# A float32 transformer kernel under a list schedule: nine landing buffers for weight blocks instead of four, other cost estimates in the planner, and mixer 1's constants asked for later

## The chip, the cores and the metric

The kernel runs on one core of one Trainium2 chip. The metric is the device time of one execution in microseconds; the figure for a kernel is the median of its runs. TensorE multiplies matrices, VectorE, ScalarE and GpSimd do the rest of the arithmetic, and SP (SyncE) issues all transfers from the chip's memory.

## The reference

The input is `x` of 256 tokens by 1024 columns, float32. Two transformer blocks follow each other. The first is a feed-forward layer (`ffn1`, gate and up of 1024 x 2816 each, silu, down 2816 x 1024), a token mixer (`mixer1`: one projection `w_in`, sliding-window attention with sinks, a pooled branch over windows of 2, 4, 8 and 16 tokens, one projection `w_out`), and a second feed-forward layer (`ffn2`). The second block is a mixer of a state-space branch (SSD) and a latent attention branch (MLA) (`mixer2`), an attention over a memory of 256 tokens (`memory`), and a feed-forward layer with a short convolution (`conv_ffn`). RMS norms stand between all of them.

```python
for l in range(DEPTH):
    h = swiglu(rms_norm(x, ffn1_pre[l]), ffn1_w_gu[l], ffn1_w_down[l])
    x = x + 0.5 * rms_norm(h, ffn1_post[l])
    h = token_mixer(rms_norm(x, mix_pre[l]), cos, sin, w_in[l], w_pool[l], ...)
    x = x + rms_norm(h, mix_post[l])
    ...
```

Some 165 MB of weights are read once each.

## The kernel before, in words

**Numbers as pairs.** A matrix product in float32 is made of three products of `float32r` numbers: each operand is split into a high part (rounded to float32r) and a low part (what is left), and high x high, high x low and low x high are added in PSUM (`mm3`, L688, and `projB`, L1074). Operands are 128 x 1024 tiles.

**Weight blocks.** `wblock` (L655) brings in one block, at most 1024 float32 a partition (512 KB): it takes a landing tile of the class `raw`, SP loads the block into it, ScalarE copies it into a high tile of the class `w` (a CAST in the profile), and VectorE subtracts to make the low tile, again of class `w` (a TENSOR_TENSOR 128x1024). When VectorE has done so, the landing tile is free. `wblocks` (L674) does this for a whole matrix strip. In the start (first strip of `ffn1`) the pieces are smaller (`CUTS`): four for gate and three for up, 256 KB each but the last, with the four loads of the transposed input `xT` (256 KB each) between.

**A planner orders everything.** The layers do not issue instructions; they call a `Plan` object, which records them as nodes with their reads and writes (`add`, L228). `schedule` (L303) is a list scheduler: it keeps an estimated time for each engine, and again and again takes the instruction that can start first, in program order among equals. `cost` (L279) estimates an instruction's duration, `HOP` (L198) the time until another engine sees the result. The result is one fixed order for each engine; `issue` (L456) writes the instructions out in that order. On the chip each engine goes through its own list in order and waits for what the next instruction needs. Some copies and scalings may run on ScalarE or VectorE; the planner chooses by its estimates.

**Buffers.** Tiles belong to classes with a fixed number of slots (`SLOTS`, L27): `w` (128 x 1024 float32, 35 of them), `raw` (the landing tiles, 4), `s` (128 x 512), `tiny`, and `ps` (8 PSUM banks). A tile gets a slot when its first instruction is scheduled and gives it back after its last. The `w` tiles also hold the transposed activations, the heads of the attention, the states, and constants such as the post-norm gains. `RESERVE` and `AHEAD` keep later tiles from taking the slots that earlier ones need; `CAP` (L31) is the most `w` tiles that weight blocks may hold in a stage. SP alone is scheduled strictly in program order: in the planner's loop it never passes a load whose slot is not there yet.

```python
if s is None:
    if e == "SP":
        break
    continue
```

**Mixer 1** (`mixer1`, L948) begins by asking for its constants: two loads of the pooling band (`band`, 512 and 256 KB), the pool weights (256 KB), the pool scale and the post-norm gain (spread over all partitions, 256 and 512 KB). They go to four `w` tiles. Three small VectorE operations prepare the sinks, the attention mask and a bf16 identity. Then come the ten blocks of `w_in` (two for key and value, four for query, four for the pool branch), the products for both halves of 128 tokens, the attention, the pool branch, the norms, and `w_out` (`down`, L765, which runs the second half of the tokens four blocks behind the first).

**Norms.** A norm's factor is a power of -0.5 of a [128, 1] tile on GpSimd (`rsq`, L709, and `rstd`, L722); ScalarE or VectorE scales with it.

Of the kernel before, what the change touches and what calls it, by code (L numbers as in the profile page):

```python
# [25 lines left out]
BLK = 1024  # L26
SLOTS = {"w": 35, "raw": 4, "s": 14, "tiny": 24, "ps": 8}  # L27
RESERVE = {"w": 4, "weights": 4, "raw": 0, "s": 3, "tiny": 6, "ps": 2}
AHEAD = {"w": 24, "weights": 4, "raw": 1000, "s": 24, "tiny": 60, "ps": 24}
CUTS = (2, 4, 6, 8), (2, 4, 8)  # L30
CAP = {"start": 22, "ffn": 22, "mix": 16, "mix2": 16, "cffn": 22}  # L31
LAG = {"ffn1": 4, "mix1": 4, "ffn2": 4, "mix2": 4, "mem": 4, "cffn": 4}
# [91 lines left out]
class View:  # L124
# [26 lines left out]
    def bitcast(self, dtype):  # L151
        return self.then(self.ix, "bitcast", dtype)

    def real(self):
        r = self.tile.real
        for op, *a in self.ops:
            if op == "get":
                r = r[a[0]]
            elif op == "rearrange":
                r = r.rearrange(a[0], **a[1])  # L160
            else:
                r = getattr(r, op)(a[0])
        return r
# [33 lines left out]
TABLES = {"Silu": 1, "Sin": 1, "Exp": 2, "Tanh": 2}  # L197
HOP = {"PE": 190.0, "ACT": 190.0, "DVE": 190.0, "POOL": 190.0, "SP": 0.0}  # L198

# [11 lines left out]
class Plan:  # L211
# [66 lines left out]
    @staticmethod  # L278
    def cost(attr, op, a, k):  # L279
        out = k.get("out", a[0] if a else None)  # L280
        size = lambda v: int(np.prod(v.shape[1:]))
        ps = any(isinstance(v, View) and v.tile.cls == "ps" for v in list(a) + list(k.values()))
        if attr == "tensor":
            if op == "transpose":
                return 109.0
            n, dt = size(out), k["rhs"].tile.dtype
            if dt == F32R:
                return 4.0 + (0.4453 * n if n >= 256 else 4 * n / 2.4)
            return 5 + max(n, P) / 2.4 * (4 if dt == F32 else 1)
        if attr == "sync" or op == "dma_start":  # L290
            n = int(np.prod(out.shape)) * 4
            return max(n / 355.0, 470.0)
        if attr == "scalar":
            return 0.833 * size(out) + 94 + (93 if "accum_out" in k else 0)
        if attr == "vector":
            if op == "reduce_max":
                return 1.04 * size(a[1]) + 70
            one = op in ("tensor_copy", "tensor_scalar") and not ps
            return (0.52 if one else 1.04) * size(out) + (130 if ps else 70)
        return 1.05 * size(out) * (2 if out.tile.dtype == F32R else 1) + 464  # L300


    def schedule(self):  # L303
# [65 lines left out]
        while left:  # L369
# [36 lines left out]
            if n.alts[e][1] == "dma_start":  # L406
                T[e] = st + (1000.0 if e == "POOL" else 60.0)
                T["BUS"] = max(T["BUS"], st) + c
                n.end = max(T["BUS"], st) + 2000
            else:  # L410
                if e == "ACT" and n.func is not None and n.func != table:
                    c += 1300 if table is not None else 0
                    table = n.func
                if e == "PE" and st > T[e] + 30:
                    c += min(213.0, c)
                T[e] = n.end = st + c
            for x in n.alts:
                known[x].remove(n)
            for t in n.tiles:
# [7 lines left out]
                else:  # L427
                    t.slot = 0
            vis = n.end + HOP[e]
            for t in n.tiles:  # L430
# [6 lines left out]
            for u in n.users:  # L437
                same = e in u.alts and len(u.alts) == 1
                u.ready = max(u.ready, n.end + (0.0 if e == "PE" and same else 130.0 if same else HOP[e]))
                u.wait -= 1  # L440
                if u.wait == 0:
                    see(u)
# [122 lines left out]
class K:  # L565
# [89 lines left out]
    def wblock(self, src):  # L655
        nc = self.nc
        _, ka, nb = src.shape
        n = ka * nb
        raw = nc.tile("raw", [P, BLK], F32)
        nc.sync.dma_start(raw[:, :n], src.rearrange("p k n -> p (k n)"))  # L660
        nc.cap = CAP[self.phase]
        hi, lo = self.w1024(F32R), self.w1024(F32R)
        nc.scalar.copy(hi[:, :n], raw[:, :n])
        nc.vector.tensor_sub(lo[:, :n], raw[:, :n], hi.bitcast(F32)[:, :n])
        nc.cap = 0
# [282 lines left out]
    def mixer1(self, xT, nxt):  # L948
        nc, a = self.nc, self.a
        self.phase = "mix"  # L950
        band = [self.w1024(), self.w1024()]
        nc.sync.dma_start(band[0], a["band"][:, :1024])
# [4 lines left out]
        psc = self.bc(pw[:, 512:], a["pool_scale"][0])  # L957
        sink = self.rows[:, :8]
        nsink = self.const("nsink", [P, 8])
        nc.vector.tensor_scalar(nsink, sink, -1.0, None, op0=ALU.mult)  # L960
        mask = self.const("mask", [P, 256], BF16)
        nc.vector.tensor_copy(mask, self.cst[:, C_SWA : C_SWA + 256])
        idb = self.const("idb", [P, P], BF16)
        nc.vector.tensor_copy(idb, self.ident)
        post = self.bc(self.w1024(), a["mix_post"][0])

        w = "w_in"
        wkv = self.wblocks(w, KD, 1024, 1280)
        wq = self.wblocks(w, KD, 512, 1024)
        wu = self.wblocks(w, KD, 0, 512)  # L970
        kvs, us, qTs = self.w1024(), self.w1024(), self.w1024()
# [644 lines left out]
```

## Time and profile before

| | |
|---|---|
| median of the runs | 1002.12 us (3 runs, 1001.24 to 1003.1) |
| profiled execution, its own time | 1004.54 us |
| profiled execution, its span | 1002.8 us, 16342 instructions |
| TensorE busy | 974.9 us (97%) |
| VectorE busy | 710.4 us (71%) |
| ScalarE busy | 519.6 us (52%) |
| GpSimd busy | 38.9 us (4%) |
| read from memory | 165.37 MB, 166 GB/s over the span |

Nearly every instruction has the same line, L469, which is where `issue` writes them all out; so the profile is read by engine, operation, shape and time, not by line. In a row of the timeline, the number in brackets is the idle time of the engine before the instruction, with what ended it. DVE is VectorE, ACT ScalarE, POOL GpSimd, PE TensorE, SPq the queue of SP.

### The profile page before, as it was taken

The numbers are of one execution on the slowest core, as the hardware profiler recorded it, in microseconds if no ns is written. First come the engines' busy times: TensorE is split into PE (matmuls) and PEld (weight loads), VectorE is DVE, ScalarE is ACT, GpSimd is POOL, SyncE is SP. The second block draws the span as 40 slices with busy tenths as digits, with TensorE's granted clock in tenths as the row PEclk, the third lists the DMA queues.
The fourth block names the chain that finished last, engine by engine and source line by source line (L and its number), as shares of the span: only waits on it lengthen the run. The fifth ranks groups of instructions, "written<-read, shape, count | busy, mean of one in ns | idle before, by whom it ended". The sixth has DMA issues, their size and how long they took to land.

```text
span 1002.8 us, 16342 instructions
## 1 busy us (share of the span) xinstructions
PE 974.9 (97%) x6437; PEld 882.1 (88%) x6437; DVE 710.4 (71%) x1201; ACT 519.6 (52%) x846; POOL 38.9 (4%) x52
## 2 busy tenths in 40 slices
PE   7999999999999999999999999999999999999997
PEld 6999998877889999888988987877997899999885
DVE  5878554567686656446999999998637698888542
ACT  5756324357455434244766666465535367555331
POOL 0100000000010000001200000111000000000000
PEclk9999999999999999999999999999999999999999
DMA  7877554455158555554444545035656056556351
GB/s 243 286 245 250 162 180 146 179 187 194 40 169 286 168 170 156 165 164 135 147 159 132 168 129 208 1 104 168 217 163 230 24 168 230 172 197 207 122 166 42
DMA packets 49421, 167.48 MB, mean 167 GB/s; under 512 B 5824, under 2 KB 7360, under 8 KB 49344
## 3 DMA queue, kind: packets, MB, share of 16 engines
q1 hardware_dynamic: 49344, 166.44, 51.3%
q8 instruction: 50, 0.82, 0.3%
q14 instruction: 27, 0.22, 0.1%
HBM read 165.37 MB, written 1.05 MB: 166 GB/s over the span
## 4 chain that ended last, share of the span: by engine, by line
PE 75%; DVE 9%; DMA 7%; ACT 4%; issue 3%; POOL 1%; SPq 0%; POOLq 0%; ACTq 0%; DVEq 0%
PE t L469 75%; DVE t L469 9%; ACT t L469 4%; DMA t<-in_w_in_from_dram 3%; DMA t<-in_ffn_w_gu_from_dram 2%; POOL t L469 1%; DMA t<-in_w_out_from_dram 1%; DMA t<-in_xT_dram 1%; SPq L469 0%; DMA t<-in_mla_w_kv_up_from_dram 0%; ACT L469 0%; POOLq L1612 0%; ACTq L469 0%; DVEq L469 0%; POOLq L469 0%
## 5 line engine op out<-in xcount | busy, mean ns | idle before, releaser
L469 PE MATMUL t<-t,t 128*128 128x256 f32 (+6 forms) x6428 | 971.4, 314 | 19.9 <-DVE t L469 11.2
L469 PEld LDWEIGHTS t<-t,t 128*128 128x128 f32 (+2 forms) x6412 | 880.0, 187 | 109.9 <-DVE t L469 16.4
L469 DVE TENSOR_TENSOR t<-t,t 128x1024 fp32r<-128x1024 f32 (+13 forms) x792 | 581.7, 777 | 240.6 <-PE t L469 121.2
L469 ACT CAST t<-t 128x1024 fp32r<-128x1024 f32 (+5 forms) x406 | 359.9, 903 | 313.1 <-PE t L469 146.6
L469 ACT ACTIVATE t<-t 128x512 bf16<-128x512 f32 (+10 forms) x132 | 72.8, 557 | 126.1 <-DVE t L469 88.7
L469 ACT ACTIVATE t<-t,t 128x256 f32<-128x256 f32 (+4 forms) x143 | 69.5, 516 | 26.0 <-POOL t L469 10.8
L469 DVE SCALAR_TENSOR_TENSOR t<-t,t,t 128x254 f32<-128x254 f32 (+5 forms) x158 | 68.6, 493 | 16.9 <-ACT t L469 12.8
L469 POOL TENSOR_TENSOR t<-t,t 128x1 f32<-128x1 f32 x38 | 33.4, 879 | 954.7 <-DVE t L469 954.7
L469 DVE CAST t<-t 128x512 fp32r<-128x512 f32 (+9 forms) x55 | 22.1, 407 | 7.8 <-PE t L469 4.7
L469 ACT COPY t<-t 128x256 f32<-128x256 f32 (+3 forms) x34 | 14.7, 446 | 12.9 <-PE t L469 12.7
L469 DVE TENSOR_SCALAR t<-t,t 128x128 f32<-128x128 f32 (+7 forms) x33 | 10.1, 317 | 14.0 <-POOL t L469 4.5
L469 DVE TENSOR_REDUCE t<-t 128x2 f32<-128x512 f32 (+1 forms) x22 | 14.4, 682 | 0.1
L469 DVE COPY t<-t 128x256 f32<-128x256 f32 (+5 forms) x27 | 13.0, 483 | 0.6 <-PE t L469 0.5
L469 DVE TENSOR_SCALAR t<-t 128x1 f32<-128x1 f32 (+5 forms) x69 | 10.1, 157 | 4.1 <-ACT t L469 2.9
L469 ACT ACTIVATION_READ_ACCUMULATOR t<-t 128x1 f32 x60 | 11.4, 190 | 0.0
L469 ACT ACTIVATION_READ_ACCUMULATOR t<-t,t 128x1 f32 x48 | 10.1, 211 | 0.0
L469 ACT ACT_TABLE_LOAD x7 | 9.0, 1283 | 1.4 <-PEq L1604 0.7
L469 DVE SCALAR_TENSOR_TENSOR t<-t,t 128x512 f32<-128x512 f32 (+2 forms) x17 | 9.2, 544 | 0.6 <-ACT t L469 0.4
L469 DVE RECIPROCAL t<-t 128x2 f32<-128x2 f32 (+2 forms) x23 | 4.0, 173 | 2.8 <-ACT t L469 2.6
L469 PEld LDWEIGHTS <-t 128*128 128x128 bf16 x25 | 2.3, 112 | 3.6 <-issue 2.1
L469 POOL COPY t<-t 128x8 f32<-128x8 f32 (+1 forms) x6 | 4.7, 810 | 4.2 <-DMA t<-in_cst_dram 3.8
L469 PE MATMUL t<-t 128*128 128x512 bf16 x9 | 3.4, 557 | 1.2 <-DVE t L469 1.2
(10 smaller groups left out, 8.1 us busy)
## 6 DMA issues: line engine op xcount, KB each, us to landing
t<-in_ffn_w_gu_from_dram SPq DMA_DIRECT2D x85, 512.0 KB, 4.9
t<-in_ffn_w_down_from_dram SPq DMA_DIRECT2D x44, 512.0 KB, 4.1
t<-in_w_ffn_up_from_dram SPq DMA_DIRECT2D x44, 512.0 KB, 4.3
t<-in_w_in_from_dram SPq DMA_DIRECT2D x34, 512.0 KB, 4.5
t<-in_w_out_from_dram SPq DMA_DIRECT2D x24, 512.0 KB, 4.5
t<-in_w_ffn_down_from_dram SPq DMA_DIRECT2D x22, 512.0 KB, 4.7
t<-in_w_mem_k_from_dram SPq DMA_DIRECT2D x8, 512.0 KB, 4.4
t<-in_w_mem_q_from_dram SPq DMA_DIRECT2D x8, 512.0 KB, 4.5
```

Source lines behind the costliest of these rows:

```text
L469: getattr(getattr(nc, attr), op)(*[real(v) for v in a], **{x: real(v) for x, v in k.items()})
```

## The change

The landing class grows from 4 to 9 tiles and `w` shrinks from 35 to 33; the cap on weight tiles goes from 22 to 20 in the start and in the feed-forward stages. The last hunk takes a scratch area for descriptors down to 1024 bytes, which no transfer of this kernel uses, and so makes room. `HOP` becomes a table by producer and consumer, and `cost` gets other constants: a scalar operand adds to a VectorE or ScalarE operation, PSUM operands are cheaper, a transfer is 413 bytes a nanosecond instead of 355, an issue on SP 420 ns instead of 60, the penalty for a gap on TensorE is gone, and a [128, 1] operation on GpSimd is 550 ns. In `mixer1` the `w_in` blocks are asked for first and the five constant loads after them. `wblock` uses a view of the landing tile in place of the tile; its instructions stay the same. The `dtype` of a view now sees a bitcast, so that the planner tells float32 products from float32r ones.

```diff
-SLOTS = {"w": 35, "raw": 4, "s": 14, "tiny": 24, "ps": 8}
+SLOTS = {"w": 33, "raw": 9, "s": 14, "tiny": 24, "ps": 8}
...
-CAP = {"start": 22, "ffn": 22, "mix": 16, "mix2": 16, "cffn": 22}
+CAP = {"start": 20, "ffn": 20, "mix": 16, "mix2": 16, "cffn": 20}
...
-HOP = {"PE": 190.0, "ACT": 190.0, "DVE": 190.0, "POOL": 190.0, "SP": 0.0}
+
+HOP = {
+    "PE": {"PE": 0.0, "ACT": 200.0, "DVE": 200.0, "POOL": 240.0, "SP": 240.0},
+    "ACT": {"PE": 155.0, "ACT": 140.0, "DVE": 133.0, "POOL": 180.0, "SP": 180.0},
+    "DVE": {"PE": 140.0, "ACT": 118.0, "DVE": 125.0, "POOL": 166.0, "SP": 166.0},
+    "POOL": {"PE": 55.0, "ACT": 33.0, "DVE": 33.0, "POOL": 40.0, "SP": 55.0},
+    "SP": {"PE": 50.0, "ACT": 30.0, "DVE": 30.0, "POOL": 30.0, "SP": 0.0},
+}
...
-            n, dt = size(out), k["rhs"].tile.dtype
+            n, dt = size(out), k["rhs"].dtype
...
-            return 5 + max(n, P) / 2.4 * (4 if dt == F32 else 1)
-        if attr == "sync" or op == "dma_start":
-            n = int(np.prod(out.shape)) * 4
-            return max(n / 355.0, 470.0)
+            return 2 * max(4 + 0.8906 * n, 109.0) if dt == F32 else 4 + 0.4453 * n
+        if op == "dma_start":
+            return max(int(np.prod(out.shape)) * 4 / 413.0, 300.0)
         if attr == "scalar":
-            return 0.833 * size(out) + 94 + (93 if "accum_out" in k else 0)
+            scalars = sum(isinstance(v, View) for v in (k.get("scale"), k.get("bias"), a[2] if op == "mul" else None))
+            return 0.833 * size(out) + (58 if ps else 94) + 88 * scalars + (98 if "accum_out" in k else 0)
...
-            return (0.52 if one else 1.04) * size(out) + (130 if ps else 70)
-        return 1.05 * size(out) * (2 if out.tile.dtype == F32R else 1) + 464
+            scalars = op in ("tensor_scalar", "scalar_tensor_tensor") and any(isinstance(v, View) for v in (a[2], a[3] if op == "tensor_scalar" else None))
+            return (0.52 if one else 1.04) * size(out) + 70 + 60 * scalars
+        return 550.0 if size(out) == 1 else 1.05 * size(out) + 464
...
-                T[e] = st + (1000.0 if e == "POOL" else 60.0)
+                T[e] = st + 420.0
...
-                if e == "PE" and st > T[e] + 30:
-                    c += min(213.0, c)
...
-            vis = n.end + HOP[e]
+            vis = n.end + 170.0
...
-                same = e in u.alts and len(u.alts) == 1
-                u.ready = max(u.ready, n.end + (0.0 if e == "PE" and same else 130.0 if same else HOP[e]))
+                u.ready = max(u.ready, n.end + max(HOP[e][x] for x in u.alts))
...
     def mixer1(self, xT, nxt):
         nc, a = self.nc, self.a
         self.phase = "mix"
+        sink = self.rows[:, :8]
+        nsink = self.const("nsink", [P, 8])
...
+        wkv = self.wblocks(w, KD, 1024, 1280)
+        wq = self.wblocks(w, KD, 512, 1024)
+        wu = self.wblocks(w, KD, 0, 512)
         band = [self.w1024(), self.w1024()]
         nc.sync.dma_start(band[0], a["band"][:, :1024])
...
         post = self.bc(self.w1024(), a["mix_post"][0])
-
-        w = "w_in"
-        wkv = self.wblocks(w, KD, 1024, 1280)
-        wq = self.wblocks(w, KD, 512, 1024)
-        wu = self.wblocks(w, KD, 0, 512)
...
-    nc = _bacc.Bacc("TRN2", target_bir_lowering=False, num_devices=1)
+    nc = _bacc.Bacc("TRN2", target_bir_lowering=False, num_devices=1, dynamic_dma_scratch_size=1024)
```

## Rows read from the trace of the kernel before

**Rows 1.** The page, busy us, share of the span and instructions by engine.

```profile
PE 974.9 (97%) x6437; PEld 882.1 (88%) x6437; DVE 710.4 (71%) x1201; ACT 519.6 (52%) x846; POOL 38.9 (4%) x52
```

**Rows 2.** Stretches: length, busy (instructions) by engine, granted clock, DMA share, GB/s.

```profile
5.97:28.23 22.26, 18.89 (x139) 17.08 (x140) 13.35 (x23) 13.15 (x23) 0.55 (x1) 1.00 0.87 284
...
208.00:212.00 4.00, 4.00 (x16) 3.29 (x15) 3.51 (x8) 3.59 (x8) 0.00 (x0) 0.59 0.61 203
...
312.00:460.00 148.00, 148.00 (x1049) 138.82 (x1048) 78.53 (x86) 55.40 (x59) 0.00 (x0) 1.00 0.56 174
...
500.00:624.00 124.00, 119.82 (x802) 108.40 (x802) 117.14 (x254) 83.63 (x184) 0.00 (x0) 1.00 0.49 159
...
985.00:1002.80 17.80, 11.05 (x48) 8.62 (x46) 2.68 (x7) 2.26 (x6) 1.10 (x2) 0.94 0.16 59
```

**Rows 3.** Waits of SP, whole span: us in total, times, longest us.

```profile
SPq L469 <- DVE t L469: 825.4, 301, 42.7
```

**Rows 4.** Timeline, 0 to 30 us: start us, us, instruction, [idle before <-releaser].

```profile
16.03 1.05 ACT L469 CAST t<-t 128x1024 fp32r<-128x1024 f32 x1 [2.42 <-DMA t<-in_ffn_w_gu_from_dram]
...
18.39 3.27 PE L469 MATMUL t<-t,t 128*128 128x256 f32 x22 [0.48 <-DVE t L469]
...
20.06 1.05 ACT L469 CAST t<-t 128x1024 fp32r<-128x1024 f32 x1 [2.98 <-DMA t<-in_ffn_w_gu_from_dram]
...
22.42 5.11 PE L469 MATMUL t<-t,t 128*128 128x256 f32 x41 [0.76 <-DVE t L469]
```

**Rows 5.** Timeline of SP alone, 150 to 236 us, issues of one source merged.

```profile
155.65 15.59 SPq L469 DMA_DIRECT2D t<-in_ffn_w_down_from_dram  x7
183.50 0.80 SPq L469 DMA_DIRECT2D t<-in_band_dram  x2
...
186.40 19.64 SPq L469 DMA_DIRECT2D t<-in_w_in_from_dram  x10
```

**Rows 6.** Waits of SP, 165 to 200 us.

```profile
SPq L469 <- PE t L469: 13.1, 2, 12.5
```

**Rows 7.** Timeline, 190 to 212 us, the entry of mixer 1.

```profile
201.26 1.05 ACT L469 CAST t<-t 128x1024 fp32r<-128x1024 f32 x1 [1.29 <-DMA t<-in_w_in_from_dram]
...
204.46 1.23 DVE L469 TENSOR_TENSOR t<-t,t 128x1024 fp32r<-128x1024 f32 x1 [0.82 <-ACT t L469]
...
207.66 4.75 PE L469 MATMUL t<-t,t 128*128 128x128 f32 x17 [2.08 <-DVE t L469]
```

**Rows 8.** Timeline, 233 to 241 us, the attention of mixer 1.

```profile
235.98 0.68 DVE L469 TENSOR_REDUCE t<-t 128x4 f32<-128x512 f32 x1
...
236.91 1.04 ACT L469 CAST t<-t 128x1024 fp32r<-128x1024 f32 x1 [1.57 <-DMA t<-in_ffn_w_gu_from_dram]
...
239.88 1.30 PE L469 MATMUL t<-t,t 128*128 128x128 f32 x5 [0.59 <-ACT t L469]
```

**Rows 9.** Timeline, 306 to 310 us, the entry of ffn2.

```profile
306.26 1.05 ACT L469 CAST t<-t 128x1024 fp32r<-128x1024 f32 x1 [0.97 <-DMA t<-in_ffn_w_gu_from_dram]
...
309.23 1.01 PE L469 MATMUL t<-t,t 128*128 128x128 f32 x7 [1.13 <-DVE t L469]
```

**Rows 10.** Waits, 500 to 630 us (mixer 2): us in total, times, longest us.

```profile
ACT t L469 <- DMA t<-in_w_in_from_dram: 8.6, 8, 2.2
PEld t L469 <- DVE t L469: 8.2, 11, 1.7
```

**Rows 11.** Timeline of mixer 2, three stops of TensorE (514:519, 560:563.5, 617:629).

```profile
517.87 1.42 PE L469 MATMUL t<-t,t 128*128 128x128 f32 x7 [1.31 <-DVE t L469]
...
562.59 1.17 PE L469 MATMUL t<-t,t 128*98 128x128 f32 x7 [0.80 <-DVE t L469]
...
619.11 2.11 PE L469 MATMUL t<-t,t 128*128 128x128 f32 x15 [0.54 <-DVE t L469]
```

**Rows 12.** Timeline, 679 to 686 us, the end of mixer 2.

```profile
679.39 3.13 POOL L469 TENSOR_TENSOR t<-t,t 128x1 f32<-128x1 f32 x1 [5.36 <-DVE t L469]
...
683.34 3.25 PE L469 MATMUL t<-t,t 128*128 128x128 f32 x11 [2.23 <-ACT t L469]
```

More of the change, by code (lines that the diff above doesn't have):

```diff
@@ L152, in bitcast, with dtype @@
         return self.then(self.ix, "bitcast", dtype)
+    @property
+    def dtype(self):
+        return ([a[0] for op, *a in self.ops if op == "bitcast"] or [self.tile.dtype])[-1]
     def real(self):
@@ L658, in wblock @@
         n = ka * nb
-        raw = nc.tile("raw", [P, BLK], F32)
-        nc.sync.dma_start(raw[:, :n], src.rearrange("p k n -> p (k n)"))
+        raw = nc.tile("raw", [P, BLK], F32)[:, :n]
+        nc.sync.dma_start(raw, src.rearrange("p k n -> p (k n)"))
         nc.cap = CAP[self.phase]
         hi, lo = self.w1024(F32R), self.w1024(F32R)
-        nc.scalar.copy(hi[:, :n], raw[:, :n])
-        nc.vector.tensor_sub(lo[:, :n], raw[:, :n], hi.bitcast(F32)[:, :n])
+        nc.scalar.copy(hi[:, :n], raw)
+        nc.vector.tensor_sub(lo[:, :n], raw, hi.bitcast(F32)[:, :n])
         nc.cap = 0
@@ L950, in mixer1 @@
         self.phase = "mix"
+        sink = self.rows[:, :8]
+        nsink = self.const("nsink", [P, 8])
+        nc.vector.tensor_scalar(nsink, sink, -1.0, None, op0=ALU.mult)
+        mask = self.const("mask", [P, 256], BF16)
+        nc.vector.tensor_copy(mask, self.cst[:, C_SWA : C_SWA + 256])
+        idb = self.const("idb", [P, P], BF16)
+        nc.vector.tensor_copy(idb, self.ident)
+        w = "w_in"
+        wkv = self.wblocks(w, KD, 1024, 1280)
+        wq = self.wblocks(w, KD, 512, 1024)
+        wu = self.wblocks(w, KD, 0, 512)
         band = [self.w1024(), self.w1024()]
@@ L957, in mixer1 @@
         psc = self.bc(pw[:, 512:], a["pool_scale"][0])
[L958 to L964, printed above, removed]
         post = self.bc(self.w1024(), a["mix_post"][0])
-        w = "w_in"
-        wkv = self.wblocks(w, KD, 1024, 1280)
-        wq = self.wblocks(w, KD, 512, 1024)
-        wu = self.wblocks(w, KD, 0, 512)
         kvs, us, qTs = self.w1024(), self.w1024(), self.w1024()
```

## The prediction

> **What bounds the kernel now.** I read the page first, then the stretches, then the waits of SP, then the timeline around each place where TensorE stood still. The page shows TensorE busy for 974.9 of 1002.8 us [rows 1]: it is the bound, and a change is worth what it does to TensorE's idle time. The stretches say where that is. In the feed-forward stages there is none: from 312 to 460 us TensorE is busy for all 148.00 us, with the DMA engines at 0.56 and VectorE and ScalarE at 78.53 and 55.40 us [rows 2]. More landing buffers or a better order can win nothing there.
>
> What can be won lies elsewhere. 1002.8 - 974.9 = 27.9 us are idle; 17.80 - 11.05 = 6.8 us of it is the end of the kernel (last residual, norm, store) [rows 2], which the change does not touch. 21.1 us remain, the launch before the first data among them, which stays as well. To this comes a price that the busy time hides. TensorE stops for 2.08 us ahead of 207.66, and the granted clock of 208 to 212 us is 0.59 [rows 2]. 0.59 over 4 us is 3.3 us at the lower level (1.2 instead of 2.4 GHz), which loses half of that, 1.65 us. I count three of these, the others behind the many small stops up to 628 us and behind the stop of 2.23 us at 683.34 that come below: 5 us. So 21.1 + 5 = 26.1 us is more than any new order can win.
>
> The cause of several stops is seen in SP. It stands 825.4 us for VectorE, in 301 waits [rows 3]: SP issues the loads strictly in order, and a landing buffer is free only when VectorE has made the low part of the block that was in it. With four buffers that ring is short. In the start the cast at 16.03 comes after 2.42 us of waiting for its transfer and the one at 20.06 after 2.98 us, and TensorE stops for 0.48 us at 18.39 and 0.76 us at 22.42 [rows 4].
>
> **The change, part by part.** The durations are of the profiled execution, which took 1004.54 us (span 1002.8); the median of the runs shown is 1002.12, so 2.4 us come off at the end.
>
> *Start.* The first group of weights is seven pieces. With nine buffers they and two blocks of the next group leave SP without a wait for VectorE, so their landing is set by the transfers alone. From 5.97 to 28.23 us these moved 284 GB/s [rows 2]; xT and the first group are 3.1 MB, 11 us at that rate, where the cast of the last piece now starts at 16.03; the next group's blocks, 0.52 MB or 1.85 us each, follow behind it without a pause. Both stops go: 0.48 + 0.76 = **-1.2 us**. At the least nothing, if the transfers, not the ring, set the pace; at the most the idle time of the stretch, 22.26 - 18.89 = 3.4 us [rows 2].
>
> *Entry of mixer 1.* SP comes to five constants (two band loads, pool weights, pool scale, post gain) ahead of the w_in blocks. Between 171.24 and 183.50 us it issues nothing [rows 5]; a wait of 12.5 us there is on TensorE [rows 6], which must give back a 1024-wide buffer for the band. The w_in blocks start at 186.40, behind the constants [rows 5]. So the cast at 201.26 waits 1.29 us for its transfer, and TensorE stops for 2.08 us at 207.66 [rows 7]. The change puts the ten w_in blocks first; they need only landing buffers, so nine of them leave SP from about 171 us on and have landed before 200. The stop goes, with its half clock: 2.08 + 1.65 = **-3.7 us**. If the casts then wait for weight buffers instead, half remains (-1.9); with the cast's own wait of 1.29 us gone too it would be -5.0.
>
> *The five loads and three small VectorE operations that move.* The loads are now queued on SP behind the tenth w_in block and ahead of w_out. Their first users, the pool products, are coded after the w_in products and sit beside the first softmax, whose maximum starts at 235.98 [rows 8]. SP was past w_in at 206.04 [rows 5], so there are 25 to 30 us of cover for 1.75 MB, which are 6.2 us at 284 GB/s. Cost 0, and the w_out blocks behind them have the same cover; were the cover gone, 6.2 us. What now hangs on them is only the band's wide buffer, which SP still waits for in order. The three conversions (sink, mask, identity) read constants that landed long ago: 0.
>
> *Attention of mixer 1.* At 236.91 a cast of an ffn2 block waits 1.57 us for its transfer; the exponentials are queued behind it on ScalarE, and TensorE stops for 0.59 us at 239.88 [rows 8]. With the block already landed: **-0.6 us** (0 to -1).
>
> *Entry of ffn2.* The cast at 306.26 waits 0.97 us for its transfer; VectorE follows, and TensorE stops for 1.13 us at 309.23 [rows 9]. The same ring: **-1.1 us** (0 to -1.3).
>
> *Mixer 2.* From 500 to 624 us VectorE is busy 117.14 of 124 us, about as full as TensorE with 119.82 [rows 2]. ScalarE waits 8.6 us for w_in transfers [rows 10], with exponentials and copies queued behind those casts. I take the three largest stops of TensorE near such waits, 1.31 + 0.80 + 0.54 = **-2.7 us** [rows 11]. They come through VectorE, so part of them may stay. The upper end is the idle time of the stretch and one half clock, 4.2 + 1.65 = -5.8 us; the lower end lies above zero and is the last rival below.
>
> *Planner's durations, 33 instead of 35 wide buffers, cap of 20.* The new costs only change the order on each engine. What that wins or loses no row shows. I bound it by the idle time that the parts above leave over (26.1 - 9.3 = 16.8 us, the launch in it) and by the last rival, and take 0, since VectorE leaves little room where the stops are. In the feed-forward stages 20 tiles are still ten blocks, and VectorE and ScalarE are half idle [rows 2]: 0.
>
> One of the new estimates can be weighed. GpSimd's [P, 1] power is given 550 ns. At 679.39 it takes 3.13 us, and TensorE stops 2.23 us at 683.34 for ScalarE [rows 12], whose work needs that power. Were 550 ns true there, stop and half clock would go, 3.9 us more. I take nothing: the changed planner still does not know of the long case. The Trainium skill, "SBUF — State Buffer", section "Who interferes with whom", says that a VectorE instruction with two SBUF inputs contends with a GpSimd instruction that reads SBUF, and that the loser fully blocks; by that rule the wait is no accident and stays wherever VectorE is full. The long power agrees with it.
>
> Sum: 1.2 + 3.7 + 0.6 + 1.1 + 2.7 = 9.3 us. 1004.5 - 9.3 = 995.2, and 2.4 less against the median: **992.8 us**.
>
> **The rivals.** (a) *Better than that*: the new order also closes stops that have nothing to do with transfers (mixer 2, memory attention, the long power). For it: 16.8 us are left. Against: VectorE is 94% busy in mixer 2. All of it would be 976, half of it is 984.4; I say 984. (b) *Less*: the extra buffers stay empty in the start and in mixer 2, because SP stands in order for wide buffers and VectorE is the bound there. Then the entries of mixer 1 and ffn2 and the one attention stop count alone: 1002.1 - 3.7 - 0.6 - 1.1 = 996.7, up to 1000. For it: the 12.5 us on TensorE; against: most of SP's waits are on VectorE. (c) *No change*: half of what (d) describes eats what the entries win: 1002. (d) *Slower*: two wide buffers less are one weight block (high and low) less. In mixer 2 the wide buffers also hold latents, states and transposed rows; a block has landed there but cannot be split until such a buffer comes free, and the split then comes late on a full VectorE by one subtraction, 1.2 us (the step at 204.46) [rows 7]. TensorE's weight loads wait for VectorE 11 times in 500 to 630 us [rows 10]. If each wait grows by 1.2 us, that is 13.2 us, plus one more half clock of 1.65, against 6.6 us won elsewhere: 1002.1 + 8.3 = 1010.4. It decides from about six of the eleven on. For it speaks VectorE's load; against it, that some of these waits come from late transfers, which the landing buffers cure.
>
> **How the numbers follow.** Forecast (987 to 996.5) 0.50, (a) 0.22, (b) 0.12, (c) 0.06, (d) 0.10. About 0.2%, 2 us, is what a measurement can tell from no change: faster by more 0.84, within it 0.06, slower 0.10. The range 980 to 1001 leaves out the far end of (a), half of (c) and (d).
>
> **What would show it.** Right: the casts of the start show no wait of 2 us for transfers; SP issues w_in from about 171 us, ahead of the band; no stop near 205 us and a granted clock of 1.00 behind it; ScalarE's waits for the weight transfers shrink everywhere. Wrong: in mixer 2 ScalarE's casts wait longer for TensorE (the wide buffers), or TensorE idles more there while VectorE's busy share falls; or the band lands after the first pool product wants it.

## The result and the profile after

The changed kernel takes **994.82 us** (median of 4 runs, 994.7 to 995.54), beside 1002.61 us (4 runs, 1001.24 to 1004.42) for the kernel before on the same chip: a ratio of 0.9923 [0.9905, 0.994], 7.8 us faster. 992.8 was predicted, within 980 to 1001. The profiled execution of after is the median one (994.82 us, span 993.0); that of before was 1.9 us above its median, so of the 9.8 us between the two spans some 2 belong to that one execution.

The page of the changed kernel, answering to [rows 1]:

```profile
PE 971.9 (98%) x6437; PEld 877.2 (88%) x6437; DVE 707.5 (71%) x1196; ACT 517.6 (52%) x851; POOL 46.0 (5%) x52
```

Idle TensorE fell from 27.9 to 993.0 - 971.9 = 21.1 us, 6.8 us less. Busy time fell by 3.0 us with the same number of matmuls. Most of that is the clock: the execution of before has three stretches at the lower clock level, near 208, 628 and 683 us (granted 0.59, 0.57 and 0.57 over 4 us, so some 1.7 us lost in each), and the changed kernel has none before its end. It is not the clock alone, since busy time rose by 0.8 us in the third and in the fourth part of the table below, at a granted clock of 1.00 in both traces. To see where, the same point of the work is looked up in both traces. Each window below begins at 0 and ends at the same place of TensorE's list (the count behind PE's busy time says so, within one); inside a part the order may differ. The kernel before, ending after ffn1, w_in, ffn2's up part, ffn2, mixer 2, and the up part of the last feed-forward; columns as in [rows 2]:

```profile
0.00:199.77 199.77, 193.87 (x1342) 178.06 (x1343) 121.61 (x182) 96.62 (x124) 4.99 (x13) 1.00 0.65 211
0.00:233.67 233.67, 225.69 (x1504) 204.50 (x1504) 145.66 (x219) 116.41 (x151) 6.24 (x16) 0.99 0.64 211
...
0.00:411.28 411.28, 401.45 (x2779) 367.52 (x2780) 263.60 (x400) 204.65 (x295) 11.81 (x25) 1.00 0.59 192
0.00:473.87 473.87, 463.88 (x3054) 418.05 (x3055) 293.84 (x440) 227.62 (x328) 14.20 (x27) 1.00 0.58 185
0.00:699.41 699.41, 680.25 (x4389) 609.11 (x4390) 503.01 (x897) 371.21 (x636) 34.44 (x47) 0.99 0.53 169
...
0.00:934.74 934.74, 913.58 (x6174) 832.76 (x6174) 683.59 (x1167) 501.69 (x822) 37.82 (x50) 0.99 0.53 172
```

The changed kernel at the same points:

```profile
0.00:197.41 197.41, 194.08 (x1342) 178.97 (x1342) 124.42 (x187) 99.34 (x127) 8.51 (x13) 1.00 0.67 227
0.00:227.92 227.92, 224.59 (x1504) 204.13 (x1504) 145.99 (x222) 115.20 (x151) 12.08 (x16) 1.00 0.67 227
...
0.00:405.30 405.30, 401.13 (x2779) 366.40 (x2780) 262.32 (x401) 200.47 (x293) 19.72 (x25) 1.00 0.60 200
0.00:470.05 470.05, 464.35 (x3053) 416.55 (x3054) 294.27 (x442) 225.68 (x329) 21.32 (x27) 1.00 0.58 191
0.00:691.96 691.96, 677.48 (x4390) 604.67 (x4390) 501.02 (x894) 372.61 (x642) 42.09 (x47) 1.00 0.53 175
...
0.00:924.75 924.75, 910.27 (x6174) 828.10 (x6175) 679.55 (x1161) 499.29 (x827) 44.87 (x50) 1.00 0.53 176
```

Differences of neighbouring rows give each part's length, and length minus PE's busy time its idle time:

| part | before, us | after, us | difference | of it idle time | predicted |
|---|---|---|---|---|---|
| start and ffn1 | 199.77 | 197.41 | -2.4 | -2.6 | -1.2 |
| w_in (entry of mixer 1) | 33.90 | 30.51 | -3.4 | -2.1 | -3.7 |
| rest of mixer 1, up part of ffn2 | 177.61 | 177.38 | -0.2 | -1.0 | -1.7 |
| down part of ffn2 | 62.59 | 64.75 | +2.2 | +1.4 | 0 |
| mixer 2 | 225.54 | 221.91 | -3.6 | -0.4 | -2.7 |
| memory layer, last up part | 235.33 | 232.79 | -2.5 | -2.0 | 0 |
| end | 68.06 | 68.25 | +0.2 | -0.1 | 0 |

**Start and entry.** Stretches of the changed kernel, columns as in [rows 2]:

```profile
5.97:28.23 22.26, 20.88 (x158) 20.60 (x159) 17.12 (x33) 16.98 (x30) 1.11 (x2) 1.00 1.01 385
25.00:50.00 25.00, 25.00 (x213) 25.00 (x212) 24.64 (x51) 22.15 (x29) 1.63 (x4) 1.00 1.03 404
199.00:235.00 36.00, 36.00 (x206) 29.61 (x206) 24.20 (x46) 20.35 (x42) 1.97 (x4) 1.00 0.65 224
...
600.00:640.00 40.00, 36.82 (x229) 31.98 (x229) 37.40 (x83) 23.38 (x58) 3.68 (x3) 1.00 0.20 66
640.00:691.96 51.96, 50.04 (x252) 40.25 (x251) 48.72 (x99) 34.76 (x65) 8.04 (x9) 1.00 0.41 138
```

and three of the kernel before:

```profile
25.00:50.00 25.00, 24.30 (x206) 24.10 (x205) 20.10 (x36) 19.94 (x31) 3.48 (x6) 1.00 0.82 286
...
628.00:632.00 4.00, 3.80 (x14) 3.32 (x15) 3.59 (x9) 1.15 (x3) 0.00 (x0) 0.57 0.00 0
...
683.00:687.00 4.00, 3.66 (x14) 3.20 (x15) 1.92 (x3) 2.02 (x4) 0.00 (x0) 0.57 0.56 195
```

In the start the transfers move 385 GB/s with nine landing buffers where with four they moved 284 [rows 2], and from 25 to 50 us 404 instead of 286. The stops at 18.39 and 22.42 us are gone; one of 1.30 us now stands at 23.49. TensorE has no idle time from 25 to 50 us, and none from 199 to 235, where the stop of 2.08 us and the clock of 0.59 stood [rows 2, 7]. **In mixer 2** the idle time hardly changed; what went are the two stretches at the lower clock level (0.57 of 4 us each, near 628 and 683), 3.2 us of busy time. After shows 1.00 there.

What ScalarE waits for in the whole span (us in total, times, longest), in the kernel before:

```profile
ACT t L469 <- DMA t<-in_ffn_w_gu_from_dram: 52.4, 47, 3.3
...
ACT t L469 <- DMA t<-in_w_in_from_dram: 20.7, 24, 2.7
```

and in the changed kernel:

```profile
ACT t L478 <- DMA t<-in_ffn_w_gu_from_dram: 2.6, 10, 0.7
```

ScalarE's waits for weight transfers have all but gone: 2.6 us are left for `w_gu`, and those for w_in, w_ffn_up and w_out, some of them in [rows 10], are no longer listed. In mixer 2 ScalarE's wait for TensorE was, in the kernel before (473.87 to 699.41 us),

```profile
ACT t L469 <- PE t L469: 29.3, 30, 2.9
```

and is, in the changed kernel (470.05 to 691.96 us),

```profile
ACT t L478 <- PE t L478: 23.7, 37, 4.0
```

The loads of SP at the entry (start, length, instruction, count), answering to [rows 5]:

```profile
161.64 28.25 SPq L478 DMA_DIRECT2D t<-in_w_in_from_dram  x10
189.98 0.86 SPq L478 DMA_DIRECT2D t<-in_band_dram  x2
```

w_in leaves from 161.64 us on, as landing buffers come free, and is out by 190; the band follows, and no engine's list of waits names the band. **The down part of ffn2** is the one place that lost. Its timeline in the changed kernel (in brackets the idle time before, and what ended it):

```profile
427.92 0.37 SPq L478 DMA_DIRECT2D t<-in_u_dram  x1
...
433.45 0.23 DVE L478 CAST t<-t 128x128 fp32r<-128x128 f32 x1 [1.43 <-DMA t<-in_u_dram]
433.59 1.22 DVE L478 TENSOR_TENSOR t<-t,t 128x1024 fp32r<-128x1024 f32 x1
...
434.86 1.42 PE L478 MATMUL t<-t,t 128*128 128x512 f32 x5 [1.14 <-DVE t L478]
```

A 0.23 us conversion of a constant of mixer 2 (`u1`) stands ahead of a weight block's subtraction on VectorE; its load was issued 5.5 us earlier and is not there. VectorE waits 1.43 us, the subtraction behind it comes late, and TensorE stops for 1.14 us. The kernel before has the same order at 449.39 us, where VectorE waits 0.76 us and TensorE does not stop.

### The profile page after: what moved, and what is told of

Same layout as the page of the kernel before. It is cut to its first block, busy times and chain, and to the rows that moved or that the text cites. A ratio compares the mean times of both kernels' runs of the same rounds, so it can differ in the third digit from the quotient of the medians.

```text
span 993.0 us, 16362 instructions
## 1 busy us (share of the span) xinstructions
PE 971.9 (98%) x6437; PEld 877.2 (88%) x6437; DVE 707.5 (71%) x1196; ACT 517.6 (52%) x851; POOL 46.0 (5%) x52
## 3 DMA queue, kind: packets, MB, share of 16 engines
HBM read 165.37 MB, written 1.05 MB: 168 GB/s over the span
## 4 chain that ended last, share of the span: by engine, by line
PE 44%; DVE 7%; issue 2%; ACT 2%; POOL 2%; POOLq 0%; DVEq 0%; ACTq 0%
PE t L478 44%; DVE t L478 7%; ACT t L478 2%; POOL t L478 2%; POOLq L1620 0%; POOLq L478 0%; DVEq L478 0%; ACTq L478 0%
## 5 line engine op out<-in xcount | busy, mean ns | idle before, releaser
L478 PEld LDWEIGHTS t<-t,t 128*128 128x128 f32 (+3 forms) x6412 | 875.1, 186 | 105.1 <-DVE t L478 12.7
L478 ACT CAST t<-t 128x1024 fp32r<-128x1024 f32 (+6 forms) x410 | 355.3, 898 | 249.1 <-PE t L478 214.3
L478 ACT ACTIVATE t<-t 128x512 f32<-128x512 f32 (+8 forms) x132 | 72.8, 557 | 142.0 <-DVE t L478 113.3
L478 POOL TENSOR_TENSOR t<-t,t 128x1 f32<-128x1 f32 x38 | 41.0, 1080 | 937.8 <-DVE t L478 937.6
L478 DVE CAST t<-t 128x512 fp32r<-128x512 f32 (+8 forms) x51 | 20.6, 406 | 8.9 <-PE t L478 5.7
L478 DVE TENSOR_SCALAR t<-t,t 128x128 f32<-128x128 f32 (+9 forms) x36 | 11.1, 316 | 16.8 <-ACT t L478 4.6
L478 DVE COPY t<-t 128x256 f32<-128x256 f32 (+4 forms) x23 | 11.5, 501 | 0.6 <-PE t L478 0.6
L478 ACT ACTIVATE t<-t,t,t 128x256 f32<-128x256 f32 x8 | 4.4, 561 | 3.2 <-DVE t L478 3.2
```

Of the source, the lines that this page charges most:

```text
L478: getattr(getattr(nc, attr), op)(*[real(v) for v in a], **{x: real(v) for x, v in k.items()})
```

## The experiments

All times are medians, with ratios to the kernel before in the same series and their 95% intervals in brackets. The kernel before took 1002.92 us in the series of `land_only`, `const_only`, `plan_only` and `four_land`, 1004.19 in that of `land_const`, `u1_early`, `four_dma_late` and `pow_slow`, and 1002.44 in that of the last four. The theory: the landing buffers win the time, the early w_in loads the entry, and the planner's durations are worth nothing. Rivals: the durations win (or lose) it; one part does it all.

**One part at a time.** `land_only`: the kernel before with only

```diff
-SLOTS = {"w": 35, "raw": 4, "s": 14, "tiny": 24, "ps": 8}
+SLOTS = {"w": 33, "raw": 9, "s": 14, "tiny": 24, "ps": 8}
-CAP = {"start": 22, "ffn": 22, "mix": 16, "mix2": 16, "cffn": 22}
+CAP = {"start": 20, "ffn": 20, "mix": 16, "mix2": 16, "cffn": 20}
-    nc = _bacc.Bacc("TRN2", target_bir_lowering=False, num_devices=1)
+    nc = _bacc.Bacc("TRN2", target_bir_lowering=False, num_devices=1, dynamic_dma_scratch_size=1024)
```

> The kernel before with nine landing buffers, 33 wide buffers, the cap of 20 and the small scratch, but with the old planner's durations and the old place of mixer 1's constants. Theory 1 (late transfers are the cause, the ring cures them): the start 1 to 2.5 us shorter, the stop at the entry of mixer 1 stays because the band's wide buffer still holds SP up, most of the 4 us that the changed kernel won in mixer 2 are there: about 996 to 998 us. Theory 2 (the planner's durations did the work): 1000 to 1003 us, with the start alone better. Theory 3 (two wide buffers fewer cost something that the other parts hide): above 1003 us.

992.64 us (990.98 to 994.73), 0.9897 [0.9866, 0.9928]: better than expected, and no slower than the whole change. Old costs, constants still in front. At the entry of mixer 1 a stop of 0.61 us is left of the 2.08. Mixer 2 is only 0.4 us shorter than before, where most of the changed kernel's gain there was expected.

`const_only`: the kernel before with only the constants of mixer 1 asked for after w_in.

```diff
-        band = [self.w1024(), self.w1024()]
...
         wu = self.wblocks(w, KD, 0, 512)
+        band = [self.w1024(), self.w1024()]
...
```

> The kernel before with only mixer 1's constants asked for after the w_in blocks. Theory 1 (the place of the five loads alone made the stop at the entry of mixer 1): 3.5 us less than before, about 998.5 to 999 us, no stop near 205 us and a granted clock of 1.00 behind it. Rival (with four landing buffers the w_in blocks cannot go ahead of TensorE either, so both parts are needed): under 2 us less.

1000.08 us (12 runs, 997.09 to 1007.2), 0.9977 [0.9953, 1.0]: 2.8 us less, with four buffers, at the edge of what the interval can tell. In its trace the stop near 205 us is gone.

`plan_only`: the kernel before with only the new durations and hops in the planner; four buffers, 35 wide ones, constants in front.

```diff
-HOP = {"PE": 190.0, "ACT": 190.0, "DVE": 190.0, "POOL": 190.0, "SP": 0.0}
+HOP = {
...
-            return max(n / 355.0, 470.0)
+            return max(int(np.prod(out.shape)) * 4 / 413.0, 300.0)
...
+        return 550.0 if size(out) == 1 else 1.05 * size(out) + 464
...
```

> The kernel before with only the planner's new durations and hops. Theory 1 (the order is worth nothing in sum): within 2 us of before, 1001 to 1004 us. Theory 2 (the durations did the work in mixer 2 and memory attention): 996 to 999 us, with the stops in memory attention near 775 us gone.

1013.84 us (1009.43 to 1025.3), 1.0118 [1.006, 1.0176]: 10.9 us slower. Neither theory had that. At the entry of mixer 1 its timeline shows

```profile
204.92 2.16 ACT L478 CAST t<-t 128x1024 fp32r<-128x1024 f32 x2 [2.13 <-DMA t<-in_w_in_from_dram]
...
209.19 3.24 PE L478 MATMUL t<-t,t 128*128 128x128 f32 x11 [5.03 <-DVE t L478]
```

a stop of 5.03 us, where the kernel before had 2.08 [rows 7]: the w_in blocks are late, and TensorE stands. This is 3 of the 9.1 us between the two profiled executions.

`four_land`: the changed kernel with four landing buffers.

```diff
-SLOTS = {"w": 33, "raw": 9, "s": 14, "tiny": 24, "ps": 8}
+SLOTS = {"w": 33, "raw": 4, "s": 14, "tiny": 24, "ps": 8}
```

> The changed kernel with four landing buffers again, all else as changed. Theory 1: what the ring gave is lost, the start back to its stops near 18 and 22 us and casts that wait for transfers in mixer 2: 998 to 1001 us. Theory 2 (the planner's durations did the work): 995 to 997 us.

1013.96 us (1012.96 to 1017.24), 1.0113 [1.0081, 1.0145]: again some 11 us slower than before, which neither theory had; under the new planner five landing buffers more are worth 19 us.

`land_const` (in the next series): buffers, caps and late constants, with the old planner; `land_only` with `const_only`'s edit. Against the changed kernel:

```diff
-HOP = {
...
+HOP = {"PE": 190.0, "ACT": 190.0, "DVE": 190.0, "POOL": 190.0, "SP": 0.0}
...
-        return 550.0 if size(out) == 1 else 1.05 * size(out) + 464
+        return 1.05 * size(out) * (2 if out.tile.dtype == F32R else 1) + 464
...
```

> The changed kernel's buffers, caps and place of mixer 1's constants, with the old planner's durations and hops. Nine buffers with the old planner and the constants in front took 992.6 us. Theory 1 (the new durations cost time at nine buffers too, as they did at four): 989 to 993 us, so 2 to 6 us below the changed kernel. Theory 2 (the new durations cost nothing once transfers land early): 994 to 996 us, like the changed kernel. The entry of mixer 1 gains little over the landing buffers alone, under 1 us, since its stop was only 1 us long there.

992.7 us (991.7 to 994.02), 0.9896 [0.9879, 0.9913]. So the parts do not add:

| planner | constants | four buffers | nine buffers |
|---|---|---|---|
| old | in front | 1002.9 (1) | 992.6 (0.9897) |
| old | later | 1000.1 (0.9977) | 992.7 (0.9896) |
| new | in front | 1013.8 (1.0118) | not run |
| new | later | 1014.0 (1.0113) | 994.8 (0.9923) |

Moving the constants wins 2.8 us with four buffers and nothing with nine: two cures for one stop. The new durations lose 11 to 14 us with four buffers and about 2 with nine; these 2 us are near what the intervals can part. At the points of the table above, `land_const` has won 9.2 us when mixer 2 begins (the changed kernel 3.8), nothing in mixer 2 itself (225.3 us long, before 225.5), and as much as the changed kernel after it. Its idle time in mixer 2 did fall, from 9.2 to 7.9 us, but it spends more of it at the lower clock level (columns as in [rows 2]):

```profile
483.00:487.00 4.00, 4.00 (x21) 3.99 (x21) 2.98 (x13) 3.57 (x9) 1.26 (x3) 0.57 0.26 91
636.00:644.00 8.00, 7.45 (x26) 5.87 (x26) 6.13 (x16) 3.60 (x8) 2.75 (x2) 0.57 0.01 2
```

0.57 over 12 us loses some 5 us, where before lost 3.4 in mixer 2 and the changed kernel nothing. So the 3.6 us of mixer 2 are the new planner's and come by the clock, paid for with 5.4 us ahead of it. This is no accident of one execution: over whole executions the six of `land_const` were granted 0.992 to 0.994 of the clock, the four of the changed kernel 0.998 to 0.999, and 0.001 of a span of 993 us is 1 us. By this estimate the new durations cost some 7 us of length with nine buffers and gave 5 back by the clock.

**Why the new durations lose.** The planner takes 1.27 us for a 512 KB block on the bus and 2.0 us more until it is there, 3.3 us in all. From issue to landing the page gives medians of 4.1 to 4.9 us for the weights of the kernel before. `four_dma_late` is `four_land` with 1.3 us more:

```diff
-                n.end = max(T["BUS"], st) + 2000
+                n.end = max(T["BUS"], st) + 3300
```

> The changed kernel with four landing buffers, in which the planner takes a transfer as 3.3 us from its turn on the bus to its landing instead of 2.0 (with 1.27 us for 512 KB this makes 4.6, where the trace shows 4.1 to 4.9 from issue to landing). With the short estimate four buffers took 1014 us. Theory 1 (the optimistic transfer made the planner put casts and what follows them too early, and engines that go in order stood behind them): 1002 to 1008 us. Rival (the other durations or the hops made the loss): 1011 to 1016 us.

998.02 us, 0.9938 [0.9904, 0.9972], better than theory 1 had it. Its 12 runs lie in two groups of six, 992.5 to 994.7 us at a granted clock of 0.996 to 0.999 and 1001.4 to 1004.6 us at 0.987 to 0.991; the clock accounts for the 9 us between them, and why it was granted less in half of the executions stays open. ScalarE's waits for transfers in `four_land`:

```profile
ACT t L478 <- DMA t<-in_ffn_w_gu_from_dram: 50.5, 51, 3.2
...
ACT t L478 <- DMA t<-in_w_in_from_dram: 15.0, 10, 3.7
```

and in `four_dma_late` (an execution of the first group):

```profile
ACT t L478 <- DMA t<-in_ffn_w_gu_from_dram: 34.2, 40, 2.5
...
ACT t L478 <- DMA t<-in_w_in_from_dram: 5.8, 7, 1.5
```

With a longer estimate the planner puts the casts later and other work ahead of them: of the 289 full-width casts, 190 stand behind more of ScalarE's other instructions than in `four_land`, 63 behind fewer. In the median 16 us come back without a buffer more. That the estimate matters is shown by this edit; that it is what made the new durations lose is not. The old planner's estimate was hardly longer (1.48 + 2.0 us), and ScalarE waited as long for transfers in the kernel before (52.4 and 20.7 us, above) as in `four_land`, which is 11 us slower. Some of the old planner's other durations were longer, some shorter; which of them the loss hangs on was not tried one by one.

`dma_late`: the same edit on the changed kernel with its nine buffers.

> The changed kernel (nine landing buffers) with the planner's transfer at 3.3 us from bus to landing instead of 2.0. With four buffers this took 1014 us to 998. Theory 1 (nine buffers land a block long before its cast, so the estimate no longer matters): within 1.5 us of the changed kernel, 993.5 to 996.5 us, with the order of constants like u1 as the only gain. Rival (the estimate matters with nine too): under 992 us.

993.69 us (992.65 to 995.64), 0.9912 [0.9892, 0.9932], 1.1 us from the changed kernel and inside its interval. With nine buffers ScalarE hardly waits for transfers (above), and the estimate hardly matters. As expected, the stop behind `u1` is gone.

`pow_slow`: the changed kernel, with GpSimd's [128, 1] power at 1600 ns in the planner.

```diff
-        return 550.0 if size(out) == 1 else 1.05 * size(out) + 464
+        return 1600.0 if size(out) == 1 else 1.05 * size(out) + 464
```

> The changed kernel in which the planner takes GpSimd's [128, 1] power as 1600 ns instead of 550. In the changed kernel these take 1.5 to 2.3 us in the state-space part, where VectorE is full, and TensorE stops 1.40, 1.02 and 0.73 us behind them. Theory 1 (the estimate is the cause of these stops): 2 to 3 us less, 992 to 993 us. Rival (the stops are in the data's own chain, and the planner has nothing to put in their place): within 1 us of the changed kernel.

987.6 us (986.77 to 989.14), 0.9845 [0.9824, 0.9866]: 7 us better than the changed kernel, more than expected. In the changed kernel the powers of mixer 2 stand in the way; its timeline:

```profile
630.05 2.27 POOL L478 TENSOR_TENSOR t<-t,t 128x1 f32<-128x1 f32 x1 [134.24 <-DVE t L478]
632.35 0.51 ACT L478 ACTIVATE t<-t,t 128x256 f32<-128x256 f32 x1 [2.22 <-POOL t L478]
...
632.91 1.28 PE L478 MATMUL t<-t,t 128*128 128x128 f32 x10 [1.40 <-ACT t L478]
```

The planner counts 550 ns for the power (the old one 1.05 + 464, so 465 ns); it takes 2.27 us, ScalarE's scaling behind it waits 2.22 us, and TensorE stops for 1.40 us; two more such stops (1.02 and 0.73 us) follow by 655 us. The waits from 615 to 690 us, changed kernel:

```profile
ACT t L478 <- POOL t L478: 10.0, 7, 2.2
...
PE t L478 <- ACT t L478: 3.2, 3, 1.4
```

and `pow_slow`:

```profile
ACT t L478 <- POOL t L478: 4.6, 5, 1.4
...
PE t L478 <- ACT t L478: 1.0, 2, 0.5
```

At the points of the table above `pow_slow` has

```profile
0.00:229.23 229.23, 224.71 (x1504) 205.14 (x1505) 146.00 (x222) 114.90 (x151) 12.07 (x16) 0.99 0.67 226
0.00:403.81 403.81, 399.29 (x2780) 367.53 (x2781) 261.64 (x400) 200.62 (x294) 19.20 (x25) 0.99 0.61 200
0.00:467.37 467.37, 461.89 (x3053) 417.77 (x3054) 292.56 (x438) 224.91 (x329) 22.50 (x27) 0.99 0.59 192
0.00:685.52 685.52, 675.13 (x4390) 605.70 (x4390) 500.81 (x897) 370.39 (x638) 44.48 (x47) 1.00 0.54 176
```

Mixer 2 is 3.8 us shorter there than in the changed kernel, nearly all of it idle time (8.8 to 4.9 us). The rest of mixer 1 with the up part of ffn2 is 2.8 us shorter, the down part of ffn2 1.2, and up to the end of w_in this execution is 1.3 us behind. Ahead of mixer 2 the order is another one too, and which of its steps win was not traced further (the stop behind `u1` is still there, 0.96 us). The powers themselves got no shorter: they average 1190 ns, 1080 in the changed kernel. What changed is what stands around them. The old planner counted them short as well, so a short power is not what the new durations brought; whether these 7 us include some of what they lost is open.

**The `u1` stop and the wide buffers.** `u1_early`: the changed kernel with the four lines that load and convert `u1` moved to the start of `rope_tables`.

```diff
     def rope_tables(self):
+        u1 = self.s512(P)
+        nc.sync.dma_start(u1, a["u1"])
+        U1 = self.U1 = self.const("U1", [P, P], F32R)
+        nc.vector.tensor_copy(U1, u1)
...
```

> The changed kernel with mixer 2's 64 KB constant u1 loaded and converted in the stage of the rope tables, long before its use. In the changed kernel VectorE stands at 433 us for this load, with a weight subtraction queued behind it, and TensorE stops 1.14 us. If the constant is the cause: no stop of TensorE in the second feed-forward's down stage and 1 to 2 us less, 993 to 994 us. Rival (the weight buffers there come free too late anyway, since the casts wait for TensorE): the stop stays and the time with it, 994.5 to 995.5 us.

993.47 us (992.87 to 994.55), 0.9904 [0.9888, 0.9921]: its interval overlaps the changed kernel's, but in the trace the stop at 434.86 us is gone, and the down part of ffn2 is 1.6 us shorter. The stop is not the new planner's. `land_const`, with nine buffers and the old durations, has it too:

```profile
428.49 0.23 DVE L469 CAST t<-t 128x128 fp32r<-128x128 f32 x1 [1.79 <-DMA t<-in_u_dram]
...
429.90 1.43 PE L469 MATMUL t<-t,t 128*128 128x512 f32 x5 [1.28 <-DVE t L469]
```

and so has `land_only` (1.26 us); in both the down part of ffn2 takes 64.4 to 64.5 us, nearly the changed kernel's 64.75. With four buffers (`const_only`, `plan_only`, `four_land`) no stop of TensorE stands behind `u1`.

`wide35`: the changed kernel with the two wide buffers given back and two landing buffers fewer, for the rival in which the wide buffers are what is short. Both numbers change at once.

```diff
-SLOTS = {"w": 33, "raw": 9, "s": 14, "tiny": 24, "ps": 8}
+SLOTS = {"w": 35, "raw": 7, "s": 14, "tiny": 24, "ps": 8}
```

> The changed kernel with 35 wide buffers and seven landing buffers, the same memory in all. If the two wide buffers were missed (the prediction's rival d), mixer 2 gets shorter and the whole takes 990 to 993 us. If seven landing buffers are too few, the start and the feed-forward entries get longer: 996 to 1000 us. If neither counts: 993.5 to 996 us.

993.29 us (992.48 to 994.61), 0.9907 [0.9888, 0.9926]. The 1.5 us against the changed kernel are not parted by the intervals; the trace shows the down part of ffn2 1.7 us shorter, without a stop of TensorE behind `u1`, and mixer 2 1.1 us longer, not shorter (a stretch at the lower clock level near 647 us, some 1.7 us; its idle time is 0.7 us less). A lack of wide buffers is not what bounds it.

**Together.** `pow_u1` has the edits of `pow_slow` and `u1_early`; `pow_dma_u1` that of `dma_late` as well.

> The changed kernel with the power on GpSimd at 1600 ns for the planner and the constant u1 fetched in the stage of the rope tables. Alone they took 987.6 and 993.5 us against the changed kernel's 994.8. Both cure different stops, so if they add up: 986 to 987 us, without a stop of TensorE near 432 us.

> As pow_u1, and the planner's transfer at 3.3 us from bus to landing. If the estimate matters with nine buffers: 983 to 985.5 us. If not: 985.5 to 988 us, like pow_u1.

986.18 us (985.63 to 986.46), 0.9835 [0.9812, 0.9858], and 985.8 us (985.73 to 986.6), 0.9833 [0.981, 0.9855]: 1.65% faster than before, twice the gain of the change. The longer transfer estimate adds nothing. The page of `pow_u1`:

```profile
PE 968.9 (98%) x6437; PEld 876.4 (89%) x6437; DVE 707.6 (72%) x1199; ACT 516.9 (53%) x848; POOL 48.2 (5%) x52
```

983.9 - 968.9 = 15.0 us are idle, 6.8 of them in the end of the kernel, behind the last up part.

## Why the prediction was right, and where it was not

The forecast case held: the sum in spans was -9.3 predicted and -9.8 measured. In medians it was -7.8, since the run profiled of before had about 2 us of its own. `land_const`, the change with the planner's durations at 0, as the sum took it, measured 992.7 us where 992.8 was predicted. That both sums came so near is in part luck, since parts too large and too small cancel. By its steps:

- *Start*: mechanism right, size too small, -1.2 against -2.4. The term counted two stops; up to 28.23 us 2.0 us of idle time went (from 3.4 to 1.4). With the two went those of 0.71, 0.60 and 0.70 us at 8.62, 11.17 and 28.23, and one of 1.30 us came at 23.49.
- *Entry of mixer 1*: right, -3.7 against -3.4: 2.1 us of idle time and 1.3 (1.65 taken) of clock. But the moved loads were not what it needed: nine buffers without them do nearly as well (`land_only`, a stop of 0.61 us left), four buffers with them too (`const_only`), and so the early issue of w_in was credited with a gain that either part makes alone.
- *Attention and entry of ffn2*: -1.7 predicted, -0.2 measured. The idle time went (-1.0 us), but busy time rose by 0.8 us. With the old durations the part is 174.5 us long, so the buffers won the term and more (3.1 us); the new durations took that back, and `pow_slow`, with another order, is as short again (174.6 us). Why it shows as busy time stays open.
- *The five loads*: 0 predicted, and no wait for them appeared. Their 1792 KB are 1.84 MB and 6.5 us at 284 GB/s, not 1.75 and 6.2; the term stays 0.
- *Down part of ffn2*: the cost of a late constant was not in the sum. It came with the nine buffers, since `land_only` and `land_const` lose as much there with the old durations; of the 2.2 us `u1_early` shows 1.1 to 1.6 us to be `u1`.
- *Mixer 2*: right size, wrong path. The three stops named were to go by landed blocks; idle time hardly moved, from 9.2 to 8.8 us. What went are two stretches at the lower clock level, which the prediction had counted in its bound of 26.1 us but left out of the sum; that the size fits is luck. `land_const` shows that the buffers alone take 1.2 us of idle time there and lose it again by the clock; the new order wins by the clock.
- *Planner's durations at 0*: this step failed. They cost 11 to 14 us with four buffers and 2 with nine, and a longer estimate of one of them, the power, wins 7 us. They were taken as 0 since "no row shows" them; rows that could have warned were there: issue to landing of 4.1 to 4.9 us beside the planner's 3.3, and a power of 3.13 us beside its 550 ns [rows 12].
- *The long power*: "the stop stays" came out in kind, not in place. The stop at 683.34 is gone, three others came. GpSimd's powers average 1080 ns in the changed kernel. By the Trainium skill, "SBUF — State Buffer", section "Who interferes with whom", the port pair that VectorE shares with GpSimd is an exclusive lock. The trace agrees: beside six subtractions of VectorE one power takes 7.15 us (last section). What planning with long powers is worth is seen in `pow_slow`, 7 us; that the wait "stays wherever VectorE is full" did not hold, since another order took most of it out of TensorE's way.
- *Rivals*: (d) fell with `wide35`. Its sign did not come either: in mixer 2 ScalarE waits 23.7 us for TensorE, 29.3 before. (b) and (c) did not come. Of (a), the memory layer's stops went (-2.0 us idle), and `land_const` has that too, so it is the buffers' doing.

## What to carry to other kernels

In a kernel whose order is fixed beforehand, depth of prefetch and truth of the estimates replace each other: nine landing buffers forgave a transfer estimate that cost 16 us (in the median) with four. The estimate that won here was nearer to the duration under load than to the smallest one in the trace, and estimates should be tried one at a time. Two orders should be compared by their granted clock as well as by their idle time. Gains of parts that cure the same stop must not be added; and the small conversion of a late constant on a full in-order engine is worth moving early.

## What the runs showed of the hardware that was not expected

GpSimd's power of 128 numbers takes 0.55 us at the least (at 638.39 us of the changed kernel, for one) and was stretched much further than the 3.13 us of [rows 12]. Three rows of the changed kernel, of VectorE and GpSimd:

```profile
192.44 6.89 DVE L478 TENSOR_TENSOR t<-t,t 128x1024 fp32r<-128x1024 f32 x6
...
192.60 7.15 POOL L478 TENSOR_TENSOR t<-t,t 128x1 f32<-128x1 f32 x1 [6.84 <-DVE t L478]
...
200.30 1.41 DVE L478 SCALAR_TENSOR_TENSOR t<-t,t,t 128x512 f32<-128x512 f32 x2 [0.90 <-POOL t L478]
```

VectorE runs six subtractions of 128x1024 without a gap, from 192.44 to 199.33. The power beside them takes 7.15 us and ends at 199.75, 0.42 us after the last of them; the next power takes 0.55 us, and it is VectorE that waits for it in the end.

The second surprise is the clock. The kernel before takes 997.8 us at a granted clock of 0.999 over the whole execution, 1002.9 at 0.996 and 1010.4 at 0.987, so most of what parts its runs is the clock. The third is the rate: with nine landing buffers the transfers move 404 GB/s over 25 us, where with four they moved 286.
